# Two-layer hybrid trunk step on one core: the value and output-gate products take the high and low weight parts side by side

## The chip, the cores and the metric

One core of a Trainium2 chip runs the whole step as one program. The metric is the device time of one execution in microseconds, and lower is better. Before the change three runs were timed: 831.06, 833.45 and 833.40 us, with a median of 833.4 us. All matrix work is on TensorE (PE in the profile), which loads a stationary operand (PEld) and streams a moving one through it; VectorE (DVE), ScalarE (ACT) and GpSimd (POOL) do the element-wise work. SBUF holds operands, and PSUM holds the sums that the matrix products leave.

## What is computed

The step has 640 tokens, 128 of context and 512 latent ones, and a model width of 1024. Layer 0 is gated attention, layer 1 a gated linear recurrence (HGRN2) with 8 heads of width 128 that runs in both directions. The change lies in layer 1 alone. Cut to what matters there:

```python
def _rec_mix(h, s0_fw, s0_bw, w_in, lb, norm_gain, w_out):
    q, f_fw, f_bw, i_in, g = jnp.split(h @ w_in, ...)   # five pieces of 1024 columns
    qh, vh = silu(heads(q)), heads(i_in)                # 8 heads of 128
    lf_fw, k_fw = gates(f_fw, lb[0])                    # log(forget), input gate
    lf_bw, k_bw = gates(f_bw, lb[1])
    o_fw, s_fw = _gla_chunked(qh, k_fw, vh, lf_fw, s0_fw)
    o_bw, s_bw = _gla_chunked(flip(qh), flip(k_bw), flip(vh), flip(lf_bw), s0_bw)
    o = rms_norm(o_fw + flip(o_bw), norm_gain)
    return (o * silu(g)) @ w_out, s_fw, s_bw
```

The value `i_in` and the output gate `g` of a head are the two projections that the change touches: 128 + 128 columns for each head.

## The kernel before

**Split products.** The result has float32 accuracy, but the products run on a rounded format. Each weight and each activation is therefore held as a high part and a low part, the low part being what the rounding left over. A product of the two takes three matrix products: high by high, high by low and low by high. `split_piece` makes the two parts of one 128 x 1024 piece of weights: ACT casts the raw piece to the high part (L242), and DVE subtracts it from the raw piece (L243). The activations of layer 1 are `h1hi` and `h1lo`.

**A head's projection.** `proj_gen(h)` issues the projection of head h. Its first part, `vg_mms`, runs over the five token tiles of 128. For each, the 128 tokens are the stationary operand, and the 256 columns of value and gate the moving one, over 8 slices `k` of the model width: three products of 256 columns for each k, 120 for a head (L1338 to L1340, output `vgps`). Then `mms` does q and the two forget gates with the weights stationary and 320 tokens moving: 6 x 24 products of 320 columns (L1348 to L1350, output `rps`). `evac_vg` brings value and gate out of PSUM after all vg products: ACT copies the value and takes the sigmoid of the gate, DVE multiplies the gate by its sigmoid, in a part of 512 columns and one of 128 (L1364).

**A head's recurrence.** `gla_gen(h)` is written as steps. Seven levels `lv` (0 to 6) each have small products on PE (L1481, L1487), followed on DVE by an update of the keys (`kv`, L1490), the product of decays (L1494) and an update of the queries (`qv`, L1495). The products of the next level read the new queries and, up to level 4, a copy `kc` of the new keys that ACT makes (L1459). After the levels come transposes `kp`, state products `sp`, output products `op` (L1544 to L1547), a norm, a gate and a transpose `oT`. The norm is a chain: ACT squares the `op` sums, DVE and POOL make the reciprocal root (`rs_t`, `rstdo`), DVE multiplies `op` by the gate (`on`, L1555) and `on` by the root (L1558). After `oT`, ACT and DVE make the high and low parts of the output (`ghi` L1565, `glo` L1566).

**How the two are interleaved.** While the projection of head h is issued, the steps of the recurrence of head h-1 are woven in by `Lane`. Each `yield` of the projection moves a clock on (1.28 for 12 vg products, 1.6 for 12 of `mms`). A step of the recurrence is issued when the clock passes its due time, which the constants set: `D_LEV` is the gap between levels, `D_GLA`, `D_KT`, `D_ST` and `D_OUT` the other gaps. So the constants, and not the chip, set how many projection products stand on PE between two steps of the recurrence. Engines run their own instructions in order, and a tile scheduler places those of DVE and ACT around the order in which they are written. `residual.step()` puts pieces of the layer's residual on POOL (tiles `rx`) while DVE works.

**Output weights.** The last head also starts to split `rec_w_out`, 8 pieces for the output projection of the tail (`wo_early`, tiles `wx`, and `tail_steps`).

Of the kernel before, what the change touches and what calls it, by code (L numbers as in the profile page):

```python
# [34 lines left out]
HALVES = ((0, 320), (320, 640))  # L35
RAW_AHEAD = 2
# [13 lines left out]
D_LEV = 2.3  # L50
# [85 lines left out]
def hybrid_step(ctx: ExitStack, tc: tile.TileContext, a: dict, o: dict):  # L136
# [97 lines left out]
    def split_piece(hi, lo, src, lo_eng=None, after=()):  # L234
        pump()
        got, raw = ahead.popleft()
        assert got == src, (got, src)
        raw = raw[:, :hi.shape[-1]]
        with ExitStack() as st:
            for ins in after:  # L240
                st.enter_context(tc.issue_after(ins))
            nc.scalar.copy(hi, raw)  # L242
            (lo_eng or nc.gpsimd).tensor_tensor(lo, raw, hi.bitcast(F32), ALU.subtract)  # L243
        pump()
# [1058 lines left out]
    def proj_gen(h, H, first):  # L1303
        loc, wvg = {}, []

        def tiles():
            H["A"] = g2.tile([P, 4 * NT], F32, tag="A", name="A")
            H["T"] = g2.tile([P, 2 * NT], F32, tag="T", name="T")
            for n in ("v", "g"):
                H[n] = g2.tile([P, NT], F32, tag=n, name=n)  # L1310
            loc["q"] = g1.tile([P, NT], F32, tag="q", name="q")

        def load(i, spare=None):
            if spare is None:
                hi = wr.tile([P, 1024], F32R, tag="whi", name="rhi")[:]
                lo = wr.tile([P, 1024], F32R, tag="wlo", name="rlo")[:]
            else:
                w = spare.tile([P, 2, 1024], F32R, tag="gate" if spare is gsp else "A", name="wspare")
                hi, lo = w[:, 0, :], w[:, 1, :]
            split_piece(hi, lo, ("rec_w_in", h, i), nc.vector)  # L1320
            return hi, lo

        def load_q(i, spare=None):
            w = load(i + 2, spare)
            loc[i] = [bank2("rps")] + [t.rearrange("p (k n) -> p k n", k=KT) for t in w]

        def load_vg(spare):
            for i in range(2):
                wvg.append([t.rearrange("p (k n) -> p k n", k=4) for t in load(i, spare if i else None)])

        def vg_mms(tt):
            if tt % 4 == 0:
                loc["vg", tt // 4] = bank2("vgps")
            out = wide(loc["vg", tt // 4])[:, tt % 4 * CW:(tt % 4 + 1) * CW]
            t = slice(tt * P, (tt + 1) * P)
            for k in range(KT):
                hi, lo = (w[:, k % 4, :] for w in wvg[k // 4])
                nc.tensor.matmul(out, h1hi[:, k, t], hi, start=(k == 0), stop=False)  # L1338
                nc.tensor.matmul(out, h1hi[:, k, t], lo, start=False, stop=False)  # L1339
                nc.tensor.matmul(out, h1lo[:, k, t], hi, start=False, stop=(k == KT - 1))  # L1340
                if k % 4 == 3:
                    yield 1.28

# [10 lines left out]
        def evac_vg():  # L1354
            s = g1.tile([P, NT], F32, tag="s", name="s")
            for i, n in ((0, 4), (1, 1)):
                pv = wide(loc["vg", i])[:, :n * CW].rearrange("p (t e d) -> p e t d", t=n, e=2)
                c = slice(i * 4 * P, (i * 4 + n) * P)

                def tok(t):  # L1360
                    return t[:, c].rearrange("p (t d) -> p t d", t=n)
                nc.scalar.copy(tok(H["v"]), pv[:, 0])
                nc.scalar.activation(tok(s), pv[:, 1], AF.Sigmoid)
                nc.vector.tensor_tensor(tok(H["g"]), pv[:, 1], tok(s), ALU.mult)  # L1364
# [27 lines left out]
        for tt in range(TS):  # L1392
            yield from vg_mms(tt)
        if first:
            load_q(0, g2)
        yield from vg_mms(TS)
        lane.finish(1)
        tiles()
        evac_vg()
# [48 lines left out]
    def gla_gen(h, H):  # L1448
        A, T, v, g = H["A"], H["T"], H["v"], H["g"]
# [76 lines left out]
        for i, c in enumerate((0, 1, 2, 4, 1, 2, 3, 4)):  # L1526
            nc.tensor.matmul(wide(sp)[:, i * P:(i + 1) * P], kt[:, i * P:(i + 1) * P], v[:, c * P:(c + 1) * P], start=True, stop=True)
# [14 lines left out]
        for c in range(TT):  # L1542
            cc = slice(c * P, (c + 1) * P)
            nc.tensor.matmul(opw[:, cc], At[:, cc], v[:, cc], start=True, stop=(c == TS))  # L1544
# [10 lines left out]
        nc.vector.tensor_tensor(on, opw[:, :NT], g, ALU.mult)  # L1555
        residual.step()
        on3 = on[:].rearrange("p (a b) -> p a b", a=TT)
# [52 lines left out]

    def wo_early():
# [3 lines left out]
        slots.extend(wr.tile([P, 1024], F32R, tag=t, name=t)[:] for t in ("whi", "wlo"))  # L1615
# [190 lines left out]
```

## The time and the profile before

| | |
|---|---|
| runs | 831.06, 833.45, 833.40 us; median 833.4 us |
| the profiled execution | 831.35 us, of which the profile's span is 829.6 us |
| granted TensorE clock | 0.995 of full speed |
| PE busy | 803.0 us, 97% of the span |
| DVE, ACT, POOL busy | 559.9, 386.8, 214.0 us |

The profile is of one execution, the program's instructions as the chip ran them. Times in it are counted from the first instruction, and L1338 is line 1338 of the kernel. A timeline row gives start, duration, engine, line, operation, output and inputs, and in brackets how long the engine had been idle and what ended that. Rows of PE show each product longer than the distance to the next, since products are pipelined: the cost of a product is the distance from its start to the start of the next. The recurrent layer's heads run from about 383 us to 750 us; before lies layer 0, after it the output projection.

### The profile page before, as it was taken

To read this page: it belongs to the slowest core of one execution; us is meant where nothing else is said; L and a number is where in the kernel's file an instruction comes from. 1 tells how busy PE (TensorE), PEld (TensorE's weight loads), DVE (VectorE), ACT (ScalarE), POOL (GpSimd) and SP (SyncE) were. 2 spreads that over 40 slices of the span, in tenths; PEclk is the share of its full clock that TensorE was granted. 3 is DMA by queue.
4 is the path that set the end of the run, shared out by engine and by line. 5 is a ranking of instruction groups with operands and counts; after the bars stand their busy time and mean duration, and the time that the engine had idled before them with its cause. 6 is when DMAs were issued, how large, how long until landed. Compare 5 with 4: busy or idle time off the path is not lost.

```text
span 829.6 us, 19207 instructions
## 1 busy us (share of the span) xinstructions
PE 803.0 (97%) x8025; PEld 725.2 (87%) x8025; DVE 559.9 (67%) x997; ACT 386.8 (47%) x783; POOL 214.0 (26%) x261
## 2 busy tenths in 40 slices
PE   8999999999999899999999999999999999999994
PEld 5789999788889676889999999999999999998774
DVE  4567767675777975775456685657667685858486
ACT  2252554575666775232444445345444444445232
POOL 0123001353344942100001324042333224021121
PEclk9999999999999999999999999999999999999997
DMA  9953244133140243511313323232413313324041
GB/s 329 396 168 131 102 153 166 66 132 125 51 129 26 72 158 100 199 58 62 102 53 104 89 64 101 70 102 71 116 58 92 101 53 98 114 69 156 24 162 76
DMA packets 34327, 93.28 MB, mean 112 GB/s; under 512 B 5041, under 2 KB 12225, under 8 KB 34241
## 3 DMA queue, kind: packets, MB, share of 16 engines
q1 hardware_dynamic: 23568, 74.10, 26.7%
q0 software_dynamic: 4768, 14.18, 5.6%
q10 hardware_dynamic: 5904, 3.78, 1.5%
q8 instruction: 63, 1.03, 0.5%
q14 instruction: 24, 0.19, 0.1%
HBM read 82.85 MB, written 9.19 MB: 111 GB/s over the span
## 4 chain that ended last, share of the span: by engine, by line
PE 86%; DVE 7%; DMA 2%; issue 2%; POOL 1%; ACT 1%; SPq 0%; DVEq 0%; ACTq 0%; POOLq 0%
PE rps L1348 7%; PE rps L1349 7%; PE rps L1350 7%; PE vgps L1338 5%; PE vgps L1340 5%; PE vgps L1339 5%; PE pot L923 4%; PE outp L1185 4%; PE outp L1187 4%; PE outp L1186 4%; PE pt L1009 4%; PE lv L1481 2%; PE acc L541 2%; PE sc L896 2%; PE sc L897 2%; PE qmm L363 2%
## 5 line engine op out<-in xcount | busy, mean ns | idle before, releaser
L1348 PE MATMUL rps<-h1hi,rhi 128*128 128x320 f32 x368 | 118.3, 321 | 0.0
L1349 PE MATMUL rps<-h1lo,rhi 128*128 128x320 f32 x368 | 113.8, 309 | 0.0
L1350 PE MATMUL rps<-h1hi,rlo 128*128 128x320 f32 x368 | 113.6, 309 | 0.0
L1002 POOL TENSOR_SCALAR p<-p,rc 128x640 f32<-128x640 f32 x64 | 56.9, 894 | 114.8 <-DVE rc L1001 97.6
L1348 PEld LDWEIGHTS rps<-h1hi,rhi 128*128 128x128 f32 x368 | 69.1, 188 | 1.3
L1349 PEld LDWEIGHTS rps<-h1lo,rhi 128*128 128x128 f32 x368 | 69.2, 188 | 0.0
L1350 PEld LDWEIGHTS rps<-h1hi,rlo 128*128 128x128 f32 x368 | 69.1, 188 | 0.0
L243 DVE TENSOR_TENSOR rlo<-raw,rhi 128x1024 fp32r<-128x1024 f32 x32 | 45.0, 1409 | 33.8 <-ACT rhi L242 33.8
L1509 POOL COPY At<-near 32x160 f32<-32x160 f32 x32 | 14.1, 439 | 195.4 <-DVE near L1471 194.4
L996 ACT ACTIVATE p<-sc,nm 128x640 f32<-128x640 f32 x64 | 51.1, 801 | 24.7 <-DVE nm L991 15.4
L991 DVE TENSOR_REDUCE nm<-sc 128x1 f32<-128x640 f32 x64 | 51.7, 816 | 12.7 <-PE sc L897 12.5
L1459 ACT COPY kc<-A 128x640 f32<-128x640 f32 x40 | 32.2, 805 | 54.6 <-DVE A L1490 50.6
L242 ACT CAST rhi<-raw 128x1024 fp32r<-128x1024 f32 x32 | 33.6, 1049 | 51.1 <-PE rps L1349 48.1
L1009 PE MATMUL pt<-small,p 128*128 128x128 f32 x320 | 49.0, 277 | 2.8 <-DVE pts L901 1.2
L1338 PE MATMUL vgps<-rhi,h1hi 128*128 128x256 f32 x180 | 51.5, 286 | 0.0
L1339 PE MATMUL vgps<-rlo,h1hi 128*128 128x256 f32 x180 | 50.9, 283 | 0.0
L1340 PE MATMUL vgps<-rhi,h1lo 128*128 128x256 f32 x180 | 50.8, 282 | 0.0
L1009 PEld LDWEIGHTS pt<-small,p 128*128 128x128 f32 x320 | 36.5, 140 | 11.6 <-issue 5.7
L896 PE MATMUL sc<-kk,X 128*128 128x320 f32 x128 | 42.4, 340 | 1.7 <-ACT p L996 1.6
L901 ACT COPY pts<-pt 128x512 f32<-128x512 f32 x64 | 36.1, 589 | 15.2 <-PE pt L1009 15.1
L1338 PE MATMUL vgps<-wspare,h1hi 128*128 128x256 f32 x140 | 41.7, 298 | 0.0
L923 PE MATMUL pot<-pts,vv 128*64 128x256 f32 x320 | 38.3, 384 | 2.1 <-DVE pts L901 2.0
(303 smaller groups left out, 2413.3 us busy)
## 6 DMA issues: line engine op xcount, KB each, us to landing
raw<-in_rec_w_in SPq DMA_DIRECT2D x40, 512.0 KB, 3.7
raw<-in_ada_m SPq DMA_DIRECT2D x16, 512.0 KB, 8.3
raw<-in_attn_w_in SPq DMA_DIRECT2D x16, 512.0 KB, 5.0
raw<-in_ada_s SPq DMA_DIRECT2D x16, 512.0 KB, 3.7
adaraw<-in_ada_c SPq DMA_DIRECT2D x11, 512.0 KB, 5.4
raw<-in_attn_w_out SPq DMA_DIRECT2D x8, 512.0 KB, 4.0
raw<-in_rec_w_out SPq DMA_DIRECT2D x8, 512.0 KB, 3.6
raw<-in_ada_c SPq DMA_DIRECT2D x5, 512.0 KB, 4.0
```

The costliest lines, as they stand in the source:

```text
L896: nc.tensor.matmul(out, X[:, h, t0:t0 + P], kk[:, c, k0:k1], start=True, stop=False)
L923: nc.tensor.matmul(pot[j * HD:(j + 1) * HD, :CW], vv[:, slot, c * HD:(c + 1) * HD], moving[j], start=first, stop=last)
L991: nc.vector.tensor_reduce(nm[:, 0:1], sc[:, :, :320], AX.XY, ALU.max, negate=True)
L996: return nc.scalar.activation(halves(p[:]), sc[:, :, :320], AF.Exp, bias=nm[:, 0:1], accum_out=su[:, 0:1])
L1002: nc.gpsimd.tensor_scalar(p, p, rs[:, 0:1], 1.0, ALU.mult, ALU.mult)
L1009: nc.tensor.transpose(pt[:, i * 256 + q * P:i * 256 + (q + 1) * P], ps[q][:, (k0 + i) * P:(k0 + i + 1) * P], ident)
L1338: nc.tensor.matmul(out, h1hi[:, k, t], hi, start=(k == 0), stop=False)
L1339: nc.tensor.matmul(out, h1hi[:, k, t], lo, start=False, stop=False)
L1340: nc.tensor.matmul(out, h1lo[:, k, t], hi, start=False, stop=(k == KT - 1))
L1348: nc.tensor.matmul(ps[:, j, :320], hi[:, k, :], h1hi[:, k, t], start=(k == 0), stop=False)
L1349: nc.tensor.matmul(ps[:, j, :320], hi[:, k, :], h1lo[:, k, t], start=False, stop=False)
L1350: nc.tensor.matmul(ps[:, j, :320], lo[:, k, :], h1hi[:, k, t], start=False, stop=(k == KT - 1))
```

## The change

The weights' high and low parts of value and gate now lie in one tile `[P, 2, 1024]`. For each token tile and k, one product multiplies the high tokens by the high and the low weights side by side (512 columns, in two pieces), and a second one multiplies the low tokens by the high weights (256 columns, added onto the left half). Two products take the place of three. PSUM then holds for each token tile 256 columns of the sum and 256 of the low weights' sum, so a PSUM tile holds two token tiles instead of four. `evac_vg(i)` adds the two: ACT copies the low half to SBUF (`low`, L1353), and DVE adds it to the other (L1355), three times a head (512, 512 and 256 columns) and as the vg products go. `gate_vg` then takes the sigmoid of the gate from SBUF (L1370) and multiplies (L1371), 640 columns each. Value and gate lie in one tile `vg`. `D_LEV` goes from 2.3 to 2.6, and the low parts of `rec_w_out` are subtracted in two halves of 512 columns. The core of the diff:

```diff
+HALF_PIECES = (slice(0, 512), slice(512, 1024))
-D_LEV = 2.3
+D_LEV = 2.6
...
-            (lo_eng or nc.gpsimd).tensor_tensor(lo, raw, hi.bitcast(F32), ALU.subtract)
+            for c in HALF_PIECES if src[0] == "rec_w_out" else (slice(None),):
+                (lo_eng or nc.gpsimd).tensor_tensor(lo[:, c], raw[:, c], hi[:, c].bitcast(F32), ALU.subtract)
...
         def vg_mms(tt):
-            if tt % 4 == 0:
-                loc["vg", tt // 4] = bank2("vgps")
-            out = wide(loc["vg", tt // 4])[:, tt % 4 * CW:(tt % 4 + 1) * CW]
+            if tt % 2 == 0:
+                loc["vg", tt // 2] = bank2("vgps")
+            out = loc["vg", tt // 2][:, tt % 2, :]
+            both = out.rearrange("p (e n) -> p e n", e=2)
             t = slice(tt * P, (tt + 1) * P)
             for k in range(KT):
-                hi, lo = (w[:, k % 4, :] for w in wvg[k // 4])
-                nc.tensor.matmul(out, h1hi[:, k, t], hi, start=(k == 0), stop=False)
-                nc.tensor.matmul(out, h1hi[:, k, t], lo, start=False, stop=False)
-                nc.tensor.matmul(out, h1lo[:, k, t], hi, start=False, stop=(k == KT - 1))
+                w = wvg[k // 4][:, :, k % 4, :]
+                last = k == KT - 1
+                if last:
+                    nc.tensor.matmul(out[:, :CW], h1lo[:, k, t], w[:, 0, :], start=False, stop=False)
+                nc.tensor.matmul(both, h1hi[:, k, t], w, start=(k == 0), stop=last)
+                if not last:
+                    nc.tensor.matmul(out[:, :CW], h1lo[:, k, t], w[:, 0, :], start=False, stop=False)
                 if k % 4 == 3:
                     yield 1.28
+
+        def evac_vg(i):
+            n = 2 if i < 2 else 1
+            if i == 0:
+                lane.finish(1)
+                H["vg"] = g2.tile([P, TT, 2, P], F32, tag="vg", name="vg")
+            ps = loc.pop(("vg", i))[:, :n, :]
+            low = g1.tile([P, 2, CW], F32, tag="low", name="low")
+            nc.scalar.copy(low[:, :n, :], ps[:, :, CW:])
+            dst = H["vg"][:, 2 * i:2 * i + n].rearrange("p t e d -> p t (e d)")
+            nc.vector.tensor_tensor(dst, ps[:, :, :CW], low[:, :n, :], ALU.add)
...
-        def evac_vg():
-            s = g1.tile([P, NT], F32, tag="s", name="s")
-            for i, n in ((0, 4), (1, 1)):
...
-                nc.scalar.copy(tok(H["v"]), pv[:, 0])
-                nc.scalar.activation(tok(s), pv[:, 1], AF.Sigmoid)
-                nc.vector.tensor_tensor(tok(H["g"]), pv[:, 1], tok(s), ALU.mult)
+        def gate_vg():
+            g = H["vg"][:, :, 1, :]
+            s = g1.tile([P, NT], F32, tag="s", name="s")[:].rearrange("p (t d) -> p t d", t=TT)
+            nc.scalar.activation(s, g, AF.Sigmoid)
+            nc.vector.tensor_tensor(g, g, s, ALU.mult)
...
         for tt in range(TS):
             yield from vg_mms(tt)
+            if tt % 2 and not first:
+                evac_vg(tt // 2)
         if first:
             load_q(0, g2)
+            for i in range(2):
+                evac_vg(i)
         yield from vg_mms(TS)
+        evac_vg(2)
         lane.finish(1)
         tiles()
-        evac_vg()
+        gate_vg()
```

Every yield of `vg_mms` now stands for 8 products where it stood for 12, so the clock of `Lane` runs faster against the products, and with the new `D_LEV` the steps of the recurrence stand in other places among them. The first place is PE at the end of a head: the last `op` products of one head's recurrence, the `rps` products behind them, and the next head's first `vgps` products. Before:

```order
L1546 MATMUL op<-S,A 128x128
L1547 MATMUL op<-S,A 128x128
L1544 MATMUL op<-v,At 128x128
L1348 MATMUL rps<-h1hi,rhi 128x320
L1349 MATMUL rps<-h1lo,rhi 128x320
L1350 MATMUL rps<-h1hi,rlo 128x320
...
L1338 MATMUL vgps<-rhi,h1hi 128x256
L1339 MATMUL vgps<-rlo,h1hi 128x256
L1340 MATMUL vgps<-rhi,h1lo 128x256
```

And after, where the lines of `rps` are 1361 to 1363 and the weights' tile is named `rw`:

```order
L1558 MATMUL op<-S,A 128x128
L1559 MATMUL op<-S,A 128x128
L1556 MATMUL op<-vg,At 128x128
L1361 MATMUL rps<-h1hi,rw 128x320
L1362 MATMUL rps<-h1lo,rw 128x320
L1363 MATMUL rps<-h1hi,rw 128x320
...
L1340 MATMUL vgps<-rw,h1hi 128x512
L1342 MATMUL vgps<-rw,h1lo 128x256
L1340 MATMUL vgps<-rw,h1hi 128x512
```

The rows left out are more `rps` products: 24 of them stand between `op` and the next head before, and 12 after, so `op` has moved towards the end of the head.

The second place is PE from level 0 (its 20 small products in one row) on, in the next head. Before:

```order
L1481 MATMUL lv<-A,kc 32x32 x20
L1338 MATMUL vgps<-wspare,h1hi 128x256
L1339 MATMUL vgps<-wspare,h1hi 128x256
L1340 MATMUL vgps<-wspare,h1lo 128x256
...
L1481 MATMUL lv<-A,kc 32x32 x20
```

And after:

```order
L1493 MATMUL lv<-A,kc 32x32 x20
L1340 MATMUL vgps<-wspare,h1hi 128x512
L1342 MATMUL vgps<-wspare,h1lo 128x256
...
L1493 MATMUL lv<-A,kc 32x32 x20
```

Between level 0 and level 1 stand 24 `vgps` products before, and 16 after, 8 of them of 512 columns.

The third place is DVE at the start of a head, from the reciprocal root of the norm (`rs_t`) to level 0's update of the queries (the second `A<-A,T`). Before:

```order
L192 TENSOR_SCALAR rs_t<-sso 128x5
L1555 TENSOR_TENSOR on<-op,g 128x640
L1558 TENSOR_TENSOR on<-on,rstdo 128x640
L243 TENSOR_TENSOR rlo<-raw,rhi 128x1024
L1378 TENSOR_SCALAR T<-s,omlb,lbt 128x640
L1382 TENSOR_TENSOR A<-q,T 128x640
L1385 TENSOR_TENSOR kd<-A 128x640
L1494 TENSOR_TENSOR Tb<-T 128x640
L1566 SCALAR_TENSOR_TENSOR glo<-oT,ngain,ghi 128x640
L1490 TENSOR_TENSOR A<-A,T 128x2x320
L1495 TENSOR_TENSOR A<-A,T 128x2x320
```

And after:

```order
L193 TENSOR_SCALAR rs_t<-sso 128x5
L1568 TENSOR_TENSOR on<-op,vg 128x640
L1570 TENSOR_TENSOR on<-on,rstdo 128x640
L1385 TENSOR_SCALAR T<-s,omlb,lbt 128x640
L1389 TENSOR_TENSOR A<-q,T 128x640
L245 TENSOR_TENSOR rw<-raw,rw 128x1024
L1392 TENSOR_TENSOR kd<-A 128x640
L1506 TENSOR_TENSOR Tb<-T 128x640
L1578 SCALAR_TENSOR_TENSOR glo<-oT,ngain,ghi 128x640
L1355 TENSOR_TENSOR vg<-vgps,low 128x512
L1502 TENSOR_TENSOR A<-A,T 128x2x320
L1507 TENSOR_TENSOR A<-A,T 128x2x320
```

The first add of the low sums (L1355) now stands ahead of level 0's key update (L1502), and the subtraction for the weights (`rw`) has moved two places back.

35 lines of the change are left out of this document (15 added, 20 removed).

## The prediction

> **What bounds the kernel now.** I read the page first: the busy shares, then the chain that ended last.
>
> ```profile
> PE 803.0 (97%) x8025; PEld 725.2 (87%) x8025; DVE 559.9 (67%) x997; ACT 386.8 (47%) x783; POOL 214.0 (26%) x261
> PE 86%; DVE 7%; DMA 2%; issue 2%; POOL 1%; ACT 1%; SPq 0%; DVEq 0%; ACTq 0%; POOLq 0%
> ```
>
> PE is busy nearly all the time and carries 86% of the chain. The change lies in the recurrent heads, so next I read the busy time by windows, one window for a head (columns: window, length, then busy time of PE, PEld, DVE, ACT and POOL).
>
> ```profile
> 559.85:606.90 47.05, 47.05 (x621) 45.54 (x620) 31.82 (x50) 21.34 (x43) 13.74 (x20) 1.00 0.31 85
> ```
>
> A head takes 47.05 us, and PE fills all of it at full clock, with DVE at 31.8 us and ACT at 21.3 us. So a head lasts as long as its products take, and any wait that reaches PE is added in full. How long a product takes is read from the timeline of PE, by the distance of the starts: a run of the narrow products of value and gate, and a run of products of 512 columns in layer 0, of which the first two and the seventh are shown.
>
> ```profile
> 512.73 0.28 PE L1338 MATMUL vgps<-rhi,h1hi 128*128 128x256 f32 x1
> 512.85 0.28 PE L1339 MATMUL vgps<-rlo,h1hi 128*128 128x256 f32 x1
> 512.97 0.28 PE L1340 MATMUL vgps<-rhi,h1lo 128*128 128x256 f32 x1
> ...
> 366.05 0.39 PE L1185 MATMUL outp<-wohi,hhi 128*128 128x512 f32 x1
> 366.27 0.40 PE L1186 MATMUL outp<-wolo,hhi 128*128 128x512 f32 x1
> ...
> 367.42 0.39 PE L1185 MATMUL outp<-wohi,hhi 128*128 128x512 f32 x1
> ```
>
> 256 columns take 0.120 us, 512 take (367.42 - 366.05) / 6 = 0.228 us, less than two narrow ones. The same timeline at a head's end and start gives 320 columns, and shows where level 0 and level 1 of the recurrence begin.
>
> ```profile
> 559.34 0.31 PE L1348 MATMUL rps<-h1hi,rhi 128*128 128x320 f32 x1
> 559.49 0.31 PE L1349 MATMUL rps<-h1lo,rhi 128*128 128x320 f32 x1
> 559.63 0.31 PE L1350 MATMUL rps<-h1hi,rlo 128*128 128x320 f32 x1
> 559.78 0.28 PE L1338 MATMUL vgps<-rhi,h1hi 128*128 128x256 f32 x1
> ...
> 567.60 0.63 PE L1481 MATMUL lv<-A,kc 128*32 128x32 f32 x40
> ...
> 571.23 0.56 PE L1481 MATMUL lv<-A,kc 128*32 128x32 f32 x40
> ```
>
> 320 columns take 0.147 us, on the line between the other two. So a product costs 0.42 ns a column and about 12 ns besides. Last I read DVE's timeline over the same stretch, since the new adds go there.
>
> ```profile
> 558.06 0.17 DVE L192 TENSOR_SCALAR rs_t<-sso 128x5 f32<-128x5 f32 x1 [4.70 <-ACT kt L1552]
> 558.14 0.82 DVE L1555 TENSOR_TENSOR on<-op,g 128x640 f32<-128x640 f32 x1
> 559.54 1.37 DVE L1558 TENSOR_TENSOR on<-on,rstdo 128x640 f32<-128x640 f32 x1 [0.59 <-POOL rstdo L193]
> 560.91 1.68 DVE L243 TENSOR_TENSOR rlo<-raw,rhi 128x1024 fp32r<-128x1024 f32 x1
> 562.52 1.05 DVE L1378 TENSOR_SCALAR T<-s,omlb,lbt 128x640 f32<-128x640 f32 x1
> 563.61 1.24 DVE L1382 TENSOR_TENSOR A<-q,T 128x640 f32<-128x640 f32 x1
> 564.77 0.81 DVE L1385 TENSOR_TENSOR kd<-A 128x640 f32<-128x640 f32 x1
> 565.51 0.81 DVE L1494 TENSOR_TENSOR Tb<-T 128x640 f32<-128x640 f32 x1
> 566.24 0.88 DVE L1566 SCALAR_TENSOR_TENSOR glo<-oT,ngain,ghi 128x640 fp32r<-128x640 f32 x1
> 568.35 0.83 DVE L1490 TENSOR_TENSOR A<-A,T 128x640 f32<-128x640 f32 x1 [1.23 <-issue]
> 570.04 0.83 DVE L1495 TENSOR_TENSOR A<-A,T 128x640 f32<-128x640 f32 x1 [0.87 <-ACT kc L1459]
> ```
>
> This is the place that matters. From `rs_t`, which waits for the squares of `op`, to `glo`, DVE works without a pause save 0.59 us for `rstdo`. Then it is idle for 1.23 us until level 0 on PE is done, does level 0's key update (568.35) and its query update (570.04), which ends at 570.87; level 1 on PE starts at 571.23. DVE, on average far from the bound, is here 1.23 us from being late.
>
> **The change part by part: fewer products.** In each of 8 heads 5 x 8 groups of three products become pairs, so 320 products go, with their columns kept. A pair costs 0.228 + 0.120 = 0.348 us against 3 x 0.120 = 0.360, so each group saves 0.012 us: 320 x 0.012 = **-3.8 us**, all on PE and so on the path. This takes layer 0's 512-column row for the new product, whose moving operand comes in two pieces of 256. No row shows that form; the bounds are 0.228 and two narrow products, 0.240, by which the saving is nothing. I take 0.228, the row of the same width. A page of the Trainium skill speaks against this part: TensorE: Matmul & The Clock Gate, section "Wait — 56ns, not 53.3ns?", puts the distance of warm products at their columns by 2.4 GHz and only about 2.5 ns besides. By that rule the estimate for 320 products is -0.8 us. The rows above give 12 ns, and the measurement decides here.
>
> **The steps of the recurrence are moved.** PE's order has 12 `rps` products between the last `op` product and the next head, and had 24. So `op`, and with it the DVE chain from `rs_t` on, comes 12 x 0.147 = 1.77 us later against the head's start. Level 0 stood behind 60 narrow products, 60 x 0.120 = 7.20 us, and stands behind 20 pairs, 20 x 0.348 = 6.96 us: 0.24 us earlier. And DVE does the first add of the low sums just ahead of level 0's key update. Its nearest row is the old gate product, which also read 512 columns from PSUM and SBUF (the groups of DVE by form, over four heads: busy time, mean ns).
>
> ```profile
> L1364 DVE TENSOR_TENSOR g<-vgps,s 128x512 f32<-128x512 f32 x4 | 2.7, 684 | 0.0
> ```
>
> 0.68 us, of which about 0.03 overlap the next operation: 0.65. So the key update is pushed by 1.77 + 0.24 + 0.65 = 2.66 us against level 0, less the idle time before it. That differs by head: 1.23 us above, in head 4, and in the others as follows (heads 2, 3, 5 and 6, then the last head, where a weight subtraction fills it).
>
> ```profile
> 474.25 0.83 DVE L1490 TENSOR_TENSOR A<-A,T 128x640 f32<-128x640 f32 x1 [0.87 <-issue]
> ...
> 521.30 0.83 DVE L1490 TENSOR_TENSOR A<-A,T 128x640 f32<-128x640 f32 x1 [2.10 <-issue]
> ...
> 615.40 0.83 DVE L1490 TENSOR_TENSOR A<-A,T 128x640 f32<-128x640 f32 x1 [1.23 <-issue]
> ...
> 662.45 0.83 DVE L1490 TENSOR_TENSOR A<-A,T 128x640 f32<-128x640 f32 x1 [2.10 <-issue]
> ...
> 708.55 1.23 DVE L243 TENSOR_TENSOR wx<-raw,wx 128x1024 fp32r<-128x1024 f32 x1 [0.21 <-ACT wx L242]
> 709.69 0.82 DVE L1490 TENSOR_TENSOR A<-A,T 128x640 f32<-128x640 f32 x1
> ```
>
> The key update is late by 1.79 us in head 2, by 1.43 in heads 4 and 5, by 0.56 in heads 3 and 6. Queued behind it are the copy `kc` on ACT, the query update, and level 1 on PE, which waits for both. Before, level 1 stood 24 products, 2.88 us, behind level 0; now 8 pairs, 2.78 us, so it starts 571.23 - 567.60 - 0.10 = 3.53 us after level 0. Its operands are ready 570.87 - 568.35 = 2.52 us after the key update starts, with 0.1 for the signal 2.62, and that starts 0.75 us (568.35 - 567.60) after level 0 when it isn't late: 3.37. The slack is 0.16 us, and what exceeds it stops PE: 1.63 us in head 2, 1.27 in heads 4 and 5, 0.40 in heads 3 and 6. In head 7 I take head 4's 1.43, and the weight subtraction, now in two halves, stands between key and query update: two times 0.65 us where DVE idled 0.87, so 0.4 more, less 0.16: 1.7. The sum is 1.63 + 2 x 1.27 + 2 x 0.40 + 1.7 = **+6.7 us**, a mean W of 1.1 us over six heads. Its bounds are W = 0.40, all heads as 3 and 6, and W = 1.7. In heads 0 and 1 the last head's chain isn't there, or level 0 has more products ahead of it; I count nothing.
>
> Why the idle times differ shows on POOL: two `rx` pairs run beside DVE in heads 4 and 5, one in heads 3 and 6.
>
> ```profile
> 559.50 0.73 POOL L1593 TENSOR_TENSOR rx<-rx,ln_g 128x256 f32<-128x256 f32 x1
> 560.31 1.21 POOL L1594 TENSOR_TENSOR rx<-rx,ln_b 128x256 f32<-128x256 f32 x1
> ...
> 657.26 0.82 DVE L1382 TENSOR_TENSOR A<-q,T 128x640 f32<-128x640 f32 x1
> ```
>
> The same operation (L1382) takes 0.82 us in head 6 and 1.24 in head 4. These pairs follow `rstdo` on POOL before and after, so I leave them where they are.
>
> **One wait goes.** In head 7 level 6 waits for DVE (the chain of waits):
>
> ```profile
> 726.97 0.51 PE lv L1487 x38
> ...
> 728.24 1.37 DVE A L1495
> ...
> 729.75 0.80 PE lv L1487 x20
> ```
>
> Twelve `rps` products behind level 5 end about 726.97 + 0.51 + 12 x 0.147 = 729.24, and level 6 starts at 729.75: 0.5 us. Now 24 products stand there, 1.77 us more, and it goes: **-0.5 us**. What is late next is the kv update behind level 6, for which `kp` waits behind 24 products; nothing comes of it.
>
> **Counted at nothing.** Three copies `low` and one sigmoid take the place of four operations on ACT, and DVE gains about 0.68 + 0.68 + 0.4 of adds and 0.82 for the gate against 0.68 + 0.28: 1.6 us a head. DVE's idle 15 us a head hide it; without that cover it would be 8 x 1.6 = 13 us. A PSUM tile is released by an add that runs long before the next tile is wanted. The weights' halves in the tail cost a start more each, some 0.1 us, beside products. Other levels keep 0.1 to 0.3 us of slack by the same reckoning.
>
> **Sum.** -3.8 - 0.5 + 6.7 = **+2.4 us**. The profiled execution took 831.35 us (span 829.6 and 1.75 around it), so its like takes 833.75. Runs came out at 831.06, 833.40 and 833.45; with the profiled one the mean is 832.3, and I put the forecast there: 832.3 + 2.4 = **834.7 us**. A measurement of this kernel can tell about 0.3%, 2.5 us, from no change. So this is no change that can be told, on the edge of slower.
>
> **Rivals.** All follow net = -4.3 + 6 W.
>
> *The chain isn't late (faster).* If POOL's pairs fall beside other work, since the subtraction now stands behind two operations of the chain, heads 2, 4, 5 and 7 save 0.4 us on each of three or four operations and W falls to about 0.1: -3.7, **828.6 us**. For it speaks that heads 3 and 6 already have 2.10 us; against it that even these are 0.56 late. It decides below W = 0.3.
>
> *Every head is late and another slack goes (slower).* All six heads wait as head 2 does, 1.63 us, and the state products `sp`, whose slack I reckon at 0.1, wait 0.2 behind an ACT queue with one more operation: 6 x 1.83 - 4.3 = +6.7, **839.0 us**. It decides from W = 1.13. For it: heads 2 and 7 do so by the rows; against: heads 3 and 6.
>
> *The wide product isn't cheaper (slower).* If two pieces cost what two products do, -3.8 falls away: +6.2, **838.5 us**. For it: no row shows the form; against: the weights' rows lie in the same partition. By the Trainium skill's 2.5 ns, named above, the estimate is +5.4.
>
> **How the numbers follow.** The forecast's mechanism has 0.60, its own range from +0.5 to +4.0 us (832.8 to 836.3), so about 0.36 within 0.3% and 0.24 slower. The faster rival has 0.20, the late heads 0.13, the wide product 0.07. So faster 0.20, same 0.36, slower 0.24 + 0.13 + 0.07 = 0.44. The range runs from 828.6, rounded to 828.5, to 838.5; it leaves out half of the first rival and most of the second.
>
> **What would show it.** In the profile after: 512-column `vgps` (L1340) 0.228 us apart from the next start, heads of 47.05 - 0.48 plus their wait: about 47.0 in heads 3 and 6 and 47.8 in 4 and 5; the key update (L1502) right behind the add (L1355) without idle time; PE idle before level 1 (L1493) with DVE's L1507 as the releaser; no wait at level 6 of head 7. It is wrong if level 1 doesn't wait, if the wait stands at another level, or if the pair of products takes 0.360 us.

## The result, and the profile after

The changed kernel took 836.68 us (median of 12 runs, 834.88 to 840.92), the kernel before 832.85 us (12 runs): a ratio of 1.0053, 95% interval 1.0035 to 1.0071, which is 4.4 us slower (the medians lie 3.8 us apart). Run again beside other kernels it had 1.0037 (1.0021 to 1.0053). The profiled execution took 834.91 us, 3.56 more than the one before. Of that 0.73 us lie ahead of the first product of the recurrent heads, where both kernels do the same work, and 2.83 us in the heads and the tail; the forecast for these was +2.4.

The page's busy shares and the chain that ended last:

```profile
PE 802.8 (96%) x7705; PEld 709.0 (85%) x7705; DVE 571.3 (69%) x1021; ACT 388.6 (47%) x783; POOL 212.5 (26%) x261
PE 78%; DVE 11%; issue 4%; POOL 2%; ACT 2%; DMA 2%; SPq 0%; ACTq 0%; DVEq 0%; POOLq 0%
```

320 products are gone, PE's busy time is as it was, and its part of the chain has fallen from 86% to 78%: waits have come onto the path. Where, the windows of heads 2, 3 and 4 show (window, length, busy time of PE, PEld, DVE, ACT and POOL, then the granted clock, the DMA share and GB/s):

```profile
465.77:514.08 48.31, 46.86 (x582) 43.27 (x580) 34.05 (x51) 21.41 (x43) 15.23 (x20) 1.00 0.27 81
514.08:560.95 46.87, 46.86 (x581) 43.26 (x580) 32.98 (x51) 21.42 (x42) 13.91 (x20) 1.00 0.31 89
560.95:608.90 47.95, 46.86 (x581) 43.27 (x580) 33.32 (x51) 21.41 (x43) 13.73 (x19) 1.00 0.29 84
```

The same work takes PE 46.86 us in each, 0.19 less than the 47.05 before, but heads 2 and 4 are longer by 1.45 and 1.09 us in which PE stands still. DVE's timeline in head 4, over the operations shown of before:

```profile
562.48 1.37 DVE L1570 TENSOR_TENSOR on<-on,rstdo 128x640 f32<-128x640 f32 x1 [0.59 <-POOL rstdo L194]
563.77 1.03 DVE L1385 TENSOR_SCALAR T<-s,omlb,lbt 128x640 f32<-128x640 f32 x1
564.83 0.83 DVE L1389 TENSOR_TENSOR A<-q,T 128x640 f32<-128x640 f32 x1
565.57 1.76 DVE L245 TENSOR_TENSOR rw<-raw,rw 128x1024 fp32r<-128x1024 f32 x1
567.25 1.35 DVE L1392 TENSOR_TENSOR kd<-A 128x640 f32<-128x640 f32 x1
568.53 0.81 DVE L1506 TENSOR_TENSOR Tb<-T 128x640 f32<-128x640 f32 x1
569.27 0.87 DVE L1578 SCALAR_TENSOR_TENSOR glo<-oT,ngain,ghi 128x640 fp32r<-128x640 f32 x1
570.06 0.67 DVE L1355 TENSOR_TENSOR vg<-vgps,low 128x512 f32<-128x512 f32 x1
570.66 0.81 DVE L1502 TENSOR_TENSOR A<-A,T 128x640 f32<-128x640 f32 x1
572.39 0.83 DVE L1507 TENSOR_TENSOR A<-A,T 128x640 f32<-128x640 f32 x1 [0.92 <-ACT kc L1471]
```

The key update (570.66) stands right behind the add (0.67 us) and has no idle time left before it. PE's timeline shows the pairs of products ahead of level 1 in head 4, and level 1 itself in heads 2, 3, 4 and 7:

```profile
478.54 0.56 PE L1493 MATMUL lv<-A,kc 128*32 128x32 f32 x40 [1.45 <-DVE A L1507]
...
525.41 0.56 PE L1493 MATMUL lv<-A,kc 128*32 128x32 f32 x40
...
571.42 0.39 PE L1340 MATMUL vgps<-rw,h1hi 128*128 128x512 f32 x1
571.65 0.28 PE L1342 MATMUL vgps<-rw,h1lo 128*128 128x256 f32 x1
571.76 0.39 PE L1340 MATMUL vgps<-rw,h1hi 128*128 128x512 f32 x1
...
573.37 0.55 PE L1493 MATMUL lv<-A,kc 128*32 128x32 f32 x40 [1.09 <-DVE A L1507]
...
717.00 0.19 PE L1493 MATMUL lv<-A,kc 128*32 128x32 f32 x1 [1.75 <-DVE A L1507]
```

The wait is behind DVE's query update L1507, as forecast. It lasts 1.45 us in head 2, 1.09 in head 4 (and in head 5), 1.75 in head 7, and isn't there in heads 3 and 6.

### The profile page after: what moved, and what is told of

The parts are those of the page before. It is cut to its first block, busy times and chain, and to the rows that moved or that the text cites. A ratio compares the mean times of both kernels' runs of the same rounds, so it can differ in the third digit from the quotient of the medians.

```text
span 833.1 us, 18565 instructions
## 1 busy us (share of the span) xinstructions
PE 802.8 (96%) x7705; PEld 709.0 (85%) x7705; DVE 571.3 (69%) x1021; ACT 388.6 (47%) x783; POOL 212.5 (26%) x261
## 4 chain that ended last, share of the span: by engine, by line
PE 78%; DVE 11%; issue 4%; POOL 2%; ACT 2%; DMA 2%; SPq 0%; ACTq 0%; DVEq 0%; POOLq 0%
PE rps L1361 7%; PE vgps L1340 7%; PE rps L1362 6%; PE rps L1363 6%; PE pot L925 4%; PE outp L1187 4%; PE outp L1189 4%; PE outp L1188 4%; PE pt L1011 4%; PE vgps L1342 3%; PE acc L543 2%; PE lv L1493 2%; PE sc L898 2%; PE sc L899 2%; PE qmm L365 2%
## 5 line engine op out<-in xcount | busy, mean ns | idle before, releaser
L1361 PE MATMUL rps<-h1hi,rw 128*128 128x320 f32 x368 | 118.4, 322 | 0.0
L1362 PE MATMUL rps<-h1lo,rw 128*128 128x320 f32 x368 | 113.7, 309 | 0.0
L1363 PE MATMUL rps<-h1hi,rw 128*128 128x320 f32 x368 | 113.6, 309 | 0.0
L1361 PEld LDWEIGHTS rps<-h1hi,rw 128*128 128x128 f32 x368 | 69.1, 188 | 1.3
L1362 PEld LDWEIGHTS rps<-h1lo,rw 128*128 128x128 f32 x368 | 69.2, 188 | 0.3
L1363 PEld LDWEIGHTS rps<-h1hi,rw 128*128 128x128 f32 x368 | 69.1, 188 | 0.0
L1340 PE MATMUL vgps<-rw,h1hi 128*128 128x512 f32 x180 | 64.8, 397 | 0.0
L1340 PE MATMUL vgps<-wspare,h1hi 128*128 128x512 f32 x140 | 55.1, 416 | 0.0
L245 DVE TENSOR_TENSOR rw<-raw,rw 128x1024 fp32r<-128x1024 f32 (+1 forms) x36 | 46.5, 1296 | 11.8 <-ACT rw L243 11.8
L1342 PE MATMUL vgps<-rw,h1lo 128*128 128x256 f32 x175 | 49.0, 280 | 0.0
L1377 ACT ACTIVATE s<-rps 128x640 f32<-128x640 f32 x24 | 16.9, 706 | 57.5 <-PE rps L1363 57.5
L356 PE MATMUL gps<-hhi,whi 128*128 128x320 f32 x128 | 40.0, 312 | 0.1
```

Of the source, the lines that this page charges most:

```text
L245: (lo_eng or nc.gpsimd).tensor_tensor(lo[:, c], raw[:, c], hi[:, c].bitcast(F32), ALU.subtract)
L1340: nc.tensor.matmul(both, h1hi[:, k, t], w, start=(k == 0), stop=last)
L1342: nc.tensor.matmul(out[:, :CW], h1lo[:, k, t], w[:, 0, :], start=False, stop=False)
L1361: nc.tensor.matmul(ps[:, j, :320], hi[:, k, :], h1hi[:, k, t], start=(k == 0), stop=False)
L1362: nc.tensor.matmul(ps[:, j, :320], hi[:, k, :], h1lo[:, k, t], start=False, stop=False)
L1363: nc.tensor.matmul(ps[:, j, :320], lo[:, k, :], h1hi[:, k, t], start=False, stop=(k == KT - 1))
```

## The experiments

The theory (theory 1) was that of the prediction: `op` nearer the head's end and the add make DVE's chain late for level 1. The rival at first was that the wide product and its evacuation cost the time wherever the steps stand. Traces are compared head by head, since heads of the same kind agree to about 0.05 us between executions, while the first 380 us, the same work in all, ended between 382.7 and 387.6 us.

**e1: the wide product with the old schedule.**

```diff
-D_LEV = 2.6
+D_LEV = 2.3
```

> The changed kernel with D_LEV back at 2.3: the wide product and its adds stay, and PE has 24 rps products behind op again. Theory 1, the wait at level 1 comes from op's move to the head's end together with the add ahead of the key update: the DVE chain is 1.77 us earlier, the key update is late by at most 0.1 us in heads 2 to 6, so no wait over 0.2 us at level 1 there, about 1.0 us in head 7, the 0.5 us at level 6 of head 7 is back, and heads 3 to 6 last 46.75 us; net -2.4 + 1.0 = -1.4 us against before, ratio 0.998. Theory 2, the wide product and the evacuation cost the time wherever the steps stand: the waits at level 1 stay over 1 us in heads 2, 4 and 5, ratio 1.004 or more.

The ratio was 1.0009 (0.9993 to 1.0024). Heads 2 to 6 lasted 46.81 to 46.83 us, with no wait: in them the rival fell. But head 7 lasted 51.39 us, against 47.45 in the kernel before. ACT's timeline, and DVE's, at its start:

```profile
705.49 0.59 ACT L1353 COPY low<-vgps 128x512 f32<-128x512 f32 x1 [1.46 <-PE vgps L1340]
709.95 1.05 ACT L243 CAST wx<-raw 128x1024 fp32r<-128x1024 f32 x1 [3.87 <-DMA raw<-in_rec_w_out]
710.90 0.29 ACT L1509 COPY near<-lv 128x160 f32<-128x160 f32 x1
711.08 0.83 ACT L1471 COPY kc<-A 128x640 f32<-128x640 f32 x1
```

```profile
703.26 1.75 DVE L245 TENSOR_TENSOR rw<-raw,rw 128x1024 fp32r<-128x1024 f32 x1
...
707.48 0.83 DVE L1502 TENSOR_TENSOR A<-A,T 128x640 f32<-128x640 f32 x1 [0.34 <-PE lv L1493]
711.02 1.29 DVE L245 TENSOR_TENSOR wx<-raw,wx 128x512 fp32r<-128x512 f32 x2 [2.71 <-ACT wx L243]
712.24 0.82 DVE L1507 TENSOR_TENSOR A<-A,T 128x640 f32<-128x640 f32 x1
```

and SP's queue of loads:

```profile
705.04 0.33 SPq L222 DMA_DIRECT2D raw<-in_rec_w_out  x1
```

The key update was in time (707.48). What was late is the first piece of the output weights: its cast stood on ACT ahead of level 1's key copy, waiting for its load. The load was issued at 705.04, when the subtraction `rw` (703.26 + 1.75) had given back a raw buffer, one of those into which a piece of weights is loaded before it is split. So the last head's wait had a cause that the prediction hadn't seen.

**e2: narrow products with the new schedule.** In the kernel before:

```diff
-D_LEV = 2.3
+D_LEV = 2.6
```

> The kernel before with D_LEV at 2.6: three narrow products as before, no adds of low sums, but 12 rps products behind op. Theory 1: the DVE chain comes 1.77 us later and uses up the idle time ahead of the key update and 0.28 us of slack: waits at level 1 of 0.6 us in head 2, 0.3 in heads 4 and 5, none in heads 3 and 6, 1.5 in head 7, and the 0.5 us at level 6 of head 7 goes; net about +2.1 us against before, ratio 1.0025. Theory 2: the schedule costs nothing by itself, no wait at level 1, ratio within 0.999 to 1.000.

The ratio was 1.0086 (1.0065 to 1.0106). Level 1 in heads 2, 4 and 7:

```profile
479.02 0.55 PE L1481 MATMUL lv<-A,kc 128*32 128x32 f32 x40 [0.69 <-DVE A L1495]
...
574.02 0.55 PE L1481 MATMUL lv<-A,kc 128*32 128x32 f32 x40 [0.33 <-DVE A L1495]
...
718.18 0.55 PE L1481 MATMUL lv<-A,kc 128*32 128x32 f32 x40 [1.80 <-DVE A L1495]
```

The waits of heads 2 and 4 are what theory 1 expected. The whole loss, 8.2 us in the trace, is four times what it expected: each head from 1 on lost about 0.26 us more (head 3: 47.31 against 47.05) where the state products `sp` come, and the tail took 84.64 us against 81.12, with a wait of 1.88 us in it that products at half clock followed. Neither is found in the changed kernel (tail 80.84 us), so this part of e2 says how badly the new `D_LEV` suits the narrow products, and nothing of the change.

**e3: the first add behind the key update.**

```diff
-            nc.vector.tensor_tensor(dst, ps[:, :, :CW], low[:, :n, :], ALU.add)
+            with ExitStack() as st:
+                if i == 0 and not first:
+                    st.enter_context(tc.issue_after(marks["kv0"]))
+                nc.vector.tensor_tensor(dst, ps[:, :, :CW], low[:, :n, :], ALU.add)
...
-            if tt % 2 and not first:
-                evac_vg(tt // 2)
+            if tt > 1 and not first:
+                evac_vg(tt - 2)
```

(`marks["kv0"]` is level 0's key update. For this the call of the first evacuation stands one token tile later; in the trace ACT's copy `low` runs 6.4 us into the head as in the changed kernel, so that ahead of level 1 only the add has moved.)

> The changed kernel with one operation moved: the first add of the low sums is held until level 0's key update has been issued, so it stands in the 0.87 us in which DVE waits for the key copy. Theory 1: the waits at level 1 fall by the add's 0.65 us, to 0.9 us in head 2, 0.5 in heads 4 and 5, none in heads 3 and 6, with head 7 about as it was; 2.1 us less than the changed kernel, ratio to before 1.003. Theory 2 (the place of the add is of no account, the wait is the norm's chain alone): the waits stay at 1.5, 1.2 and 1.2 us, ratio 1.005.

The ratio was 0.9990 (0.9976 to 1.0005). Level 1 in heads 2, 4 and 7:

```profile
477.69 0.55 PE L1498 MATMUL lv<-A,kc 128*32 128x32 f32 x40 [0.87 <-DVE A L1514]
...
571.82 0.55 PE L1498 MATMUL lv<-A,kc 128*32 128x32 f32 x40 [0.51 <-DVE A L1514]
...
714.50 0.55 PE L1498 MATMUL lv<-A,kc 128*32 128x32 f32 x40 [1.48 <-DVE A L1514]
```

The waits fell by 0.58 us, from 1.45 and 1.09, nearly the add's length: one operation's place on an engine that is busy 69% of the time is worth that much in each of three heads. Heads 2, 4, 5 and 7 are 2.1 us shorter together than in the changed kernel, the sum that theory 1 expected; the ratio, 0.9990, is lower than the 1.003 that it expected.

**e4: the wide product in one piece.** The two weight parts of a k were laid side by side.

```diff
-            split_piece(w[:, 0, :], w[:, 1, :], ("rec_w_in", h, i), nc.vector)
+            if i < 2:
+                w = w[:].rearrange("p e n -> p (e n)").rearrange("p (k e n) -> p k e n", k=4, e=2)
+                split_piece(w[:, :, 0, :], w[:, :, 1, :], ("rec_w_in", h, i), nc.vector)
```

> The changed kernel with the value and gate weights laid out so that the 256 high and the 256 low columns of a k lie side by side: the wide product streams 512 elements in one piece instead of two. Theory 1a, the two pieces make the wide product 0.236 us instead of layer 0's 0.228: now 0.228, a pair of products 0.347 instead of 0.354, 0.3 us less in each head, 2.3 us less in all, ratio to before 1.0025. Theory 1b, the pieces cost nothing: the wide product stays at 0.236 us, and the ratio at 1.005. The waits at level 1 are as in the changed kernel in both, longer by 0.06 us where products ahead got shorter.

PE's timeline at a head's start:

```profile
562.94 0.39 PE L1347 MATMUL vgps<-rw,h1hi 128*128 128x512 f32 x1
563.17 0.28 PE L1349 MATMUL vgps<-rw,h1lo 128*128 128x256 f32 x1
563.29 0.40 PE L1347 MATMUL vgps<-rw,h1hi 128*128 128x512 f32 x1
```

A pair takes 0.35 us, as in the changed kernel, and the heads are equal to 0.02 us (48.29, 46.86, 47.94 us for heads 2 to 4). The two pieces cost nothing that shows. The ratio of 1.0017 (1.0005 to 1.0030) is lower than the changed kernel's, with an interval that overlaps that of its second measurement; the trace gives no reason for a difference.

**e5: the changed kernel again,** beside e6 to e8.

> The changed kernel, unaltered, as the yardstick for the three kernels that run beside it, since ratios taken on different days and chips differ by some 0.2%. All theories expect the heads as they were, 48.3, 46.9, 47.9, 47.9 and 46.9 us for heads 2 to 6, and a ratio to before between 1.002 and 1.0055.

The ratio was 1.0037; heads 2 to 6 lasted 48.25, 46.81, 47.93, 47.94 and 46.82 us.

**e6: e1 with the output weights held back.** The split of `wx` is queued behind level 2's key copy and level 1's query update:

```diff
-        split_piece(hi, lo, ("rec_w_out", nh, i), nc.vector)
+        split_piece(hi, lo, ("rec_w_out", nh, i), nc.vector, marks.pop("hold", ()))
```

> The changed kernel with D_LEV at 2.3, as in e1, and the first split of the output weights (wx) held, on ACT behind level 2's key copy and on DVE behind level 1's query update of the last head. Theory 1: the 2.7 us wait at level 1 of head 7 in e1 was ACT standing at the cast of wx, whose load comes late, with the key copy queued behind it; held, the wait falls under 0.3 us, the stretch at half clock behind it goes too, head 7 lasts 47.6 us instead of 51.4, and the kernel is 3.8 us below e1 and about 2.5 us below before: ratio 0.997. Theory 2, head 7 waits for DVE's chain and not for the load: over 1 us of wait stays at level 1, ratio 1.000 or more.

The ratio was 0.9951 (0.9932 to 0.9970). The windows of heads 6 and 7:

```profile
652.80:699.60 46.80, 46.80 (x581) 43.21 (x580) 33.35 (x52) 21.67 (x42) 13.86 (x21) 1.00 0.32 88
699.60:746.40 46.80, 46.80 (x581) 43.21 (x580) 34.55 (x56) 22.41 (x43) 13.55 (x18) 1.00 0.30 93
```

Head 7 lasted 46.83 us instead of 51.39: the load of `wx`, queued ahead of the key copy, was its cause. With no wait left, the wide product is faster than the narrow ones.

**e7: the same hold with D_LEV at 2.6.**

> The changed kernel with D_LEV at 2.6 and the same hold of wx. Theory 1: in head 7 the load of wx and DVE's chain end close together, so that the wait at level 1 falls only from 1.9 us to the 1.2 us of heads 4 and 5, which have two rx pairs as it has: 0.7 us less than the changed kernel beside it. Theory 2 (DVE alone): the wait stays at 1.9 us.

The ratio was 1.0016 (0.9999 to 1.0032). Level 1 of head 7:

```profile
715.37 0.55 PE L1497 MATMUL lv<-A,kc 128*32 128x32 f32 x40 [1.09 <-DVE A L1511]
```

1.09 us instead of 1.75, the same as in heads 4 and 5: this is what the chain costs when the load is out of the way, and 0.66 us is what the load and the two subtractions behind it add. The two causes overlap, so their shares don't add up: e8 shows the load without the chain.

**e8: POOL's residual step moved.**

```diff
         nc.scalar.copy(kt, wide(kp))
+        residual.step()
         yield D_KT
...
-        residual.step()
         nc.vector.tensor_tensor(on3, on3, view(rstd, 0, [[1, TT], [0, P]]), ALU.mult)
```

> The changed kernel with the second residual step of a head moved from behind the output gate (on) to behind the kp copy, so that POOL's rx pairs no longer run beside DVE's chain at the head's end. Theory 1, these pairs stretch the chain and make heads 2, 4 and 5 differ from 3 and 6: the product by the reciprocal root takes 0.82 us instead of 1.37, the waits at level 1 fall from 1.5, 1.2 and 1.2 us under 0.2, heads 2 to 6 last 46.9 us, head 7's wait falls by about 1 us as the weights' subtraction ends sooner: 4.5 us less than the changed kernel beside it, ratio to before 0.998. Theory 2, the chain is late by the move of op and the add alone: operations and waits stay within 0.3 us of the changed kernel's.

The ratio was 0.9946 (0.9930 to 0.9962). DVE's timeline in a head, the steps that the prediction put down to contention:

```profile
565.00 0.83 DVE L1570 TENSOR_TENSOR on<-on,rstdo 128x640 f32<-128x640 f32 x1 [0.59 <-POOL rstdo L194]
565.74 0.61 DVE L1385 TENSOR_SCALAR T<-s,omlb,lbt 128x640 f32<-128x640 f32 x1
...
567.13 1.22 DVE L245 TENSOR_TENSOR rw<-raw,rw 128x1024 fp32r<-128x1024 f32 x1
568.26 0.82 DVE L1392 TENSOR_TENSOR kd<-A 128x640 f32<-128x640 f32 x1
...
571.86 0.83 DVE L1502 TENSOR_TENSOR A<-A,T 128x640 f32<-128x640 f32 x1 [0.65 <-PE lv L1493]
```

1.37, 1.03, 1.76 and 1.35 us became 0.83, 0.61, 1.22 and 0.82, together 2.0 us, and the key update has 0.65 us of idle time before it although `op` and the add are where the change put them. Heads 1 to 6 have no wait (46.80 us each from head 2 on). So POOL's `rx` pairs beside DVE are the third part of the cause, and one that can be moved at no cost that shows. Head 7 still waited 1.5 us, where a fall by about 1 us was expected. Its chain was in time too (0.65 us of idle time before the key update at 712.26), but the cast of `wx` waited for its load until 713.67 with the key copy behind it: the load, with the cast and the subtractions behind it, costs 1.5 us without the chain, the chain 1.1 without the load (e7), and both together 1.75.

**e10: e7 and e8 together.**

> The changed kernel with D_LEV at 2.6, the residual step moved as in e8 and wx held as in e7: both causes of the waits are taken away with the steps of the recurrence where the change put them. Theory 1: no wait over 0.2 us in heads 2 to 7, heads of 46.8 us, 1.5 us less than e8 in head 7, ratio to before 0.995 to 0.997, as e6. Theory 2, something else in the late place of op costs time: heads over 46.9 us or a wait at another level, ratio over 0.998.

The ratio was 0.9960 (0.9942 to 0.9978), and heads 2 to 7 lasted 46.80 us each, without a wait on PE. e6, e8 and e10 all beat both kernels, the one before by 3.3 to 4.5 us; their intervals don't tell them apart. By the traces they lie 2.9, 1.2 and 2.9 us below the kernel before.

**e9 and e11: what a wait costs behind it.** e1's head 7 had lost 4.6 us with a wait of 2.5 at level 1 and one of 0.3 at level 6. DVE was given small products ahead of level 0's key update, in e6's kernel, so that PE stood still for a chosen time:

```diff
+                for n in range(STALLS.get(h, 0) if lev == 0 else 0):
+                    d = nc.vector.tensor_tensor(At[:, :32 * TT], pt[:, :32 * TT], A[:, :32 * TT], ALU.mult)
+                    st.enter_context(tc.issue_after(d.ins))
```

> The kernel of e6 with a wait made on purpose: in heads 2 to 6 DVE does 11, 13, 15, 17 and 20 small products of 160 columns (their output is overwritten later) between level 0 and its key update, so that PE stands still at level 1 for a time that grows by about 0.5 us from head to head, from 1 to 4 us. Theory 1: a pause of PE costs more than its length from about 2.5 us on, since e1 (2.8 us) and the tail of e2 showed products at twice their distance behind a pause, and the changed kernel (2.1 us) did not; so behind the shorter waits the granted clock stays at 1.00 and behind the longer ones it is 0.5 for about 3 us, some 1.5 us lost each. Theory 2, the slow products of e1 and e2 had another cause (a transfer, another engine): the granted clock is 1.00 behind every wait, and a head lasts 46.8 us and its wait.

In the one execution of e9 PE stood still for 2.5, 3.9 and more, up to 6.4 us, longer than the 1 to 4 us that were meant, so that no short wait was among them; all five were followed by products at twice their distance. The window from level 1 on in head 2 (the figure behind the five busy times is the granted clock):

```profile
480.40:482.90 2.50, 2.38 (x45) 2.16 (x46) 1.56 (x3) 0.65 (x1) 0.00 (x0) 0.50 0.03 7
```

e11 has shorter waits, since the length at which the clock begins to fall is still open.

> As e9, with shorter waits: 9 to 11 of the small products, with one of 32 columns besides in heads 3 and 5, so that PE stands idle at level 1 for about 1.8 to 2.5 us in steps of 0.2. If the clock falls with the length of a pause, the shortest of them keep 1.00 behind them, as the changed kernel's 1.9 us did, and the longest are followed by about 3 us at 0.5, as e9's 2.5 us was; the step between them is looked for. If it falls by the moment of the pause and not by its length, short and long ones are mixed.

The waits, again of one execution, came out at 2.4 us in three heads and 2.5 in two, not from 1.8 on, since the scheduler had also put the second add of low sums, which waits for later products, ahead of level 0's query update. PE's level 1 in heads 2, 3 and 5:

```profile
483.21 0.55 PE L1498 MATMUL lv<-A,kc 128*32 128x32 f32 x40 [2.39 <-DVE A L1516]
...
534.00 0.56 PE L1498 MATMUL lv<-A,kc 128*32 128x32 f32 x40 [2.38 <-DVE A L1516]
...
634.37 0.76 PE L1498 MATMUL lv<-A,kc 128*32 128x32 f32 x40 [2.53 <-DVE A L1516]
```

Behind the same wait of 2.4 us the clock fell in heads 2 and 3, and not in head 4 (2.39 us, ending at 584.77). The record of the granted clock shows why. Each stretch at half clock in the heads lasts 3.41 us, or 6.83, and within an execution these stretches begin a whole number of 3.41 us apart: at 484.02, 535.22, 634.20 and 685.40 us in e11 (15, 29 and 15 times), at 480.27, 531.47, 586.08, 637.28 and 691.89 in e9. So in these executions the clock changes on a grid of 3.41 us, whatever the program does at that moment. Heads 2, 3 and 4 on this grid, for each the window that holds the pause, or most of it, and the next:

```profile
480.61:484.02 3.41, 1.02 (x42) 0.77 (x42) 2.23 (x4) 1.29 (x2) 0.00 (x0) 1.00 0.00 0
484.02:487.43 3.41, 3.41 (x12) 2.90 (x11) 2.01 (x4) 1.75 (x2) 0.00 (x0) 0.50 0.02 5
531.81:535.22 3.41, 1.23 (x44) 1.13 (x45) 2.64 (x4) 1.18 (x2) 0.00 (x0) 1.00 0.00 0
535.22:538.63 3.41, 3.41 (x13) 2.93 (x11) 2.29 (x5) 1.77 (x2) 0.00 (x0) 0.50 0.00 0
583.01:586.42 3.41, 1.65 (x46) 1.50 (x47) 3.07 (x5) 0.89 (x3) 0.00 (x0) 1.00 0.03 5
586.42:589.83 3.41, 3.41 (x59) 3.00 (x58) 2.77 (x5) 1.98 (x3) 0.00 (x0) 1.00 0.00 0
```

PE was idle for 2.39 and 2.18 us of the first two windows, and half clock followed. In head 4 the grid divides the pause, 1.76 us remain in one window, and the clock stays.

**Traces and ratios side by side.** From the first product of head 0 to the end of the execution, against the kernel before, and the measured ratios:

| kernel | difference in the trace, us | as a ratio | ratio measured |
|---|---|---|---|
| changed | +2.83 | 1.0034 | 1.0053, 1.0037 |
| e1 | +1.65 | 1.0020 | 1.0009 |
| e2 | +8.21 | 1.0099 | 1.0086 |
| e3 | +0.64 | 1.0008 | 0.9990 |
| e4 | +2.99 | 1.0036 | 1.0017 |
| e6 | -2.93 | 0.9965 | 0.9951 |
| e7 | +2.12 | 1.0025 | 1.0016 |
| e8 | -1.21 | 0.9985 | 0.9946 |
| e10 | -2.91 | 0.9965 | 0.9960 |

Both put the kernels in nearly the same order. In e8, and less so in e3 and e4, the measured ratio is lower than the trace gives, in the changed kernel higher; the cause stays open (e8's ratio rests on five executions).

## Why the prediction was right, and where its steps were off

**The place and the mechanism: right.** Level 1 waits behind the query update, with the key update right behind the add. In heads 2 to 6 it is the sum 1.77 + 0.24 + 0.65 us less the idle time: e1 (steps back, no wait) takes away the 1.77, e3 (add moved, 0.58 us less) the 0.65, and e8 (POOL moved, no wait) makes the idle time larger; the wait goes or shrinks by about that part.

**The waits, head by head.** Against an undisturbed head of 46.80 us, heads 2 to 6 are longer by 1.51, 0.07, 1.15, 1.13 and 0.05 us, where 1.63, 0.40, 1.27, 1.27 and 0.40 were forecast. The reckoning holds to 0.15 us where `rx` pairs run in twos; in heads 3 and 6 it gave 0.33 to 0.35 too much. The traces show two small errors in it. The key update starts 0.51 us after `glo` ends, not 0.65, since the operations overlap. And `glo` ends 1.65 us later against the head's start in head 3 and 1.85 in head 4, where I put 1.77 for both: POOL's pairs stayed, but DVE's order behind them changed, so that in head 4 they now stretch `T`, the subtraction and `kd`, by 0.2 us more than the three operations of before.

**Head 7: right size, half of the cause.** I forecast 1.7 us by the chain and DVE's two halves; it is 1.8, and that this is near is luck. The chain alone costs 1.1 (e7); the load of `wx`, which I left out, costs 1.5 alone, with the cast and the subtractions behind it (e8). In the changed kernel the halves do stand between key and query update, but after 0.60 us in which DVE waits for the cast, and the cast for the load. The step that failed is the subtraction `rw`: I followed it on DVE only, and it also gives back the raw buffer for which the next load waits. Before, it ended at 703.8 in a head that starts at 701.0; after, at 710.1 in one that starts at 703.7. The issues on SP's queue, first before, then after:

```profile
703.85 6.28 SPq L221 DMA_DIRECT2D raw<-in_rec_w_out  x2
```

```profile
710.11 0.33 SPq L222 DMA_DIRECT2D raw<-in_rec_w_out  x1
```

**The saving: mis-sized.** -3.8 us was forecast, 0.48 a head. An undisturbed head lasts 46.80 us (e6, e10) against 47.05, so 0.25 us; heads 0 and 1 gained 0.33 and 0.31, head 6, which was 47.13 before, 0.33, and head 7 0.2 without its wait at level 6. Over all heads that is some -2.2 us, about 7 ns for a product saved instead of 12. I took layer 0's 0.228 us for the new product; it took 0.234. Pairs that nothing interrupts are 0.351 us apart on average, not 0.348, and vary from 0.340 to 0.361; three narrow products took 0.359. e4 excludes the two pieces as the reason; the runs don't show another. The Trainium skill's 2.5 ns (TensorE: Matmul & The Clock Gate, section "Wait — 56ns, not 53.3ns?") is too small by 4 ns, my 12 was too large by 5; here the measurement decides.

**The rest.** The wait at level 6 of head 7 is gone, as forecast, but it was shorter than I reckoned: the level began 0.4 us later than in the other heads, not 0.5. The tail is 0.28 us shorter, for which I had nothing. Together -2.2 - 0.4 - 0.3 + 5.7 (waits) = +2.8 us, the 2.83 of the two traces. The two errors, 1.6 us too much saved and 1.0 us too much waited, partly cancel; that the sum is nearer than its terms is luck. The time measured over many runs, +4.4 and +3.1 us, lies above the traces' +2.8, which is just under the first interval (2.9 to 5.9) and inside the second (1.8 to 4.4). So 836.68 us lies a little above what I gave for the forecast's own mechanism (832.8 to 836.3).

**The rivals.** In the first, late chains were to vanish if POOL's pairs fell beside other work: they didn't move by themselves, but e8, which moves them, does just that. The second, every head as head 2, did not come, and `sp` lost nothing in the changed kernel (0.26 us a head in e2). The third, a wide product that saves nothing, is true in part: 1.6 of the 3.8 us aren't there.

## What to carry to other kernels

Where one engine is full, the cost of an edit elsewhere is not its length but its length less the idle time ahead of the next operation that the full engine waits for; read that idle time from the timeline at each such place, since a mean share (DVE 67%) says nothing of it. When a schedule moves an operation, follow also what it releases: a buffer given back late starts a load late, and an in-order queue passes that on to whatever stands behind the load's first user. Before giving up a change that costs waits, look for the work that merely shares the time, like the residual step here: moving it took the waits out of heads 2 to 6, and with the load held as well the same change gained 0.4% (e10) instead of losing 0.4 to 0.5%.

## What the runs showed of the hardware

**A pause of TensorE can cost more than its length.** Pauses of PE in the heads of up to 1.86 us (e4's head 7, and 1.75 in the changed kernel) were followed by products at full clock; of pauses of 2.38 or 2.39 us two of three, and all of 2.5 us and more (e1, e9 and e11), by a granted clock of 0.5 for 3.41 or 6.83 us. In the tail of e2 a pause of 1.88 us, soon after one of 0.25, was followed by half clock too. In e1 the last head, 51.39 us instead of 46.8, lost some 1.5 us this way besides its two waits. What counts, by these traces, is the idle time within one window of 3.41 us: in the heads and the tail's recurrence 2.03 us (e2) and more were followed by half clock, 1.86 us (e4) and less were not. That bound is this stage's own: at about 6 and 290 us, under other work, windows with 1.1 to 1.7 us of idle time were followed by half clock too. The Trainium skill (TensorE: Matmul & The Clock Gate, section "What's actually happening") tells of an activity monitor with a free-running window of about 3.4 us that grants half the clock after an idle window. The traces agree on the window and that it runs freely, but here some 2 us of idle time in it were enough, a window idle from end to end was not needed.

**POOL stretches DVE.** With `rx` pairs on POOL beside them, operations of DVE took 0.4 to 0.5 us longer (1.37 against 0.83 us, 1.76 against 1.22), and in e8 all of them fell back at once.

**The same program varies in its first part.** The first 380 us, the same work in each kernel, ended at 382.7 to 387.6 us; stretches at half clock are a part of that (none in the kernel before, which ended at 382.8, 10.2 us of them in e8, at 387.6), not the whole (3.4 us in e4, at 385.5, and in e9, at 383.0). Executions of one kernel differed by 7 us, the fastest with the highest mean granted clock and the slowest with the lowest (0.996 with 834.49 us, 0.985 with 841.46 in e5). Differences of 2 us between kernels are read from traces by stage, or from a dozen runs.
